# Seven half-size products in place of eight in two of the six gate/up blocks of each FFN

## The chip, the core and the metric

One core of a Trainium2 chip runs the whole program in one launch. The metric is the device time in microseconds (us). The engines are TensorE (PE in the profile: matmuls, with weight loads on a row of their own, PEld), VectorE (DVE), ScalarE (ACT), GpSimd (POOL) and SyncE (SP), whose queue issues the DMA transfers.

## The reference

Two layers, each of an FFN, a mixer and a second FFN, on 256 tokens of width 1024. The inner width of an FFN is 2816.

```python
def swiglu(h, w_gate, w_up, w_down):
    return (jax.nn.silu(h @ w_gate) * (h @ w_up)) @ w_down

for l in range(DEPTH):
    f1 = swiglu(rmsnorm(x, g[0]), ffn_w_gate[l, 0], ffn_w_up[l, 0], ffn_w_down[l, 0])
    x = x + 0.5 * rmsnorm(f1, g[1])
    m = hybrid_mixer(rmsnorm(x, g[2]), ...)   # S5 scan, chunk attention, gates
    x = x + rmsnorm(m, g[3])
    f2 = swiglu(rmsnorm(x, g[4]), ffn_w_gate[l, 1], ffn_w_up[l, 1], ffn_w_down[l, 1])
    x = x + 0.5 * rmsnorm(f2, g[5])
```

## The kernel before

The 256 tokens are two tiles of 128. All weights stream from DRAM once, in 368 chunks of 128 x 1024 fp32 (512 KB each). `weight` brings a chunk in: a DMA into a `raw` buffer, an ACT copy to `wh` in a format with fewer bits that PE reads (L358), and a DVE subtraction `wl` = `raw` - `wh` (L365), whose two inputs both lie in SBUF. A product of fp32 quality is then three matmuls: high by high, high by low and low by high. `mm_two_k` does this for a chunk that holds two 128-row pieces of a 512-wide block: six matmuls 128x512 (L400). Both token tiles use each chunk, tile 1 some three chunks after tile 0 (`LAG`).

An FFN goes through its inner width in blocks, `N_BLK`: five of 512 and one of 256. For a block of 512 a tile takes four gate chunks and four up chunks, 24 matmuls each; DVE multiplies the up result with the SiLU of the gate result, `t_split` transposes it on PE (L414) and splits it into high and low, and `gemm_wide` takes it through the four down chunks of the block before, into two PSUM banks per tile that hold the FFN's output until the end.

The order is no hand-written one: `Kern` records operations with an estimated cost, and `Graph.schedule` places them by due times (a clock of `TAU` per half chunk, less `MARGIN` for work of another stream) and by free buffers. `SLOTS` is the number of buffers of each kind. On each engine instructions then run strictly in that order. GpSimd does little: some memsets, and the power -1/2 of the norms (`pow`, L376, 128x1). Small work for the mixer (`prep`) is strewn over the first FFN of a layer, or over the FFN in front of it.

Of the kernel before, what the change touches and what calls it, by code (L numbers as in the profile page):

```python
# [12 lines left out]
F32 = mybir.dt.float32  # L13
# [7 lines left out]
P = 128  # L21
# [8 lines left out]
N_BLK = (512, 512, 512, 512, 512, 256)  # L30
FFN_CHUNKS = 66
# [4 lines left out]
SLOTS = {"blk": 28, "ps": 8, "wh": 8, "wl": 8, "raw": 4, "gain": 2,  # L36
# [4 lines left out]
MARGIN = {"conv": 7.558, "conv0": 3.423, "task": 7.748, "att0": 37.576, "s50": 37.749, "att1": 28.585, "s51": 29.753, "prep": 111.598}  # L41
# [20 lines left out]
class View:  # L62
# [249 lines left out]
class Kern:  # L312
    def __init__(self, g, x, g0, gains, wall, sp, bias, out):
# [4 lines left out]
        self.chunk = [0, 0]  # L318
        self.last_raw = None
# [46 lines left out]

    def copy(self, out, a):
# [24 lines left out]
    def mm(self, out, lhsT, rhs, start, stop):  # L392
        n, m = rhs.free_size(), lhsT.free_size()
        if rhs.dt == F32R:
            cost = n / 2370
        elif m == 32:
            cost = 0.05
        else:
            cost = max(0.2, n / 592)
        return self.g.op("pe", cost, [out], [lhsT, rhs], lambda: self.nc.tensor.matmul(  # L400
            out.ap(), lhsT=lhsT.ap(), rhs=rhs.ap(), start=start, stop=stop))
# [40 lines left out]

    def weight(self, i):
        if i not in self.ws:
# [3 lines left out]
            raw = g.buf("raw", [P, 1024])  # L448
            wh, wl = g.buf("wh", [P, 1024], F32R), g.buf("wl", [P, 1024], F32R)
            parts = [slice(0, 512), slice(512, 1024)] if i < 2 else [slice(0, 1024)]  # L450
            for s in parts:
                self.last_raw = self.dma(raw[:, s], self.w_d[i][:, s], after=[self.last_raw] if self.last_raw else [])
            for s in parts:
                self.act(wh[:, s], raw[:, s], AF.Copy)
                self.tt(wl[:, s], raw[:, s], wh[:, s].bitcast(F32), ALU.subtract)
            self.ws[i] = (wh, wl)
# [3 lines left out]
    def take(self, t):  # L460
# [16 lines left out]
    def gemm(self, t, xs):
# [6 lines left out]
        return bank  # L484

# [658 lines left out]
```

## Time and profile before

| | |
|---|---|
| time, median of 3 runs | 1153.3 us (1153.28 to 1153.45) |
| span of the profiled execution, first to last instruction | 1151.6 us |
| granted TensorE clock | 0.999 of full speed |
| PE busy | 1140.8 us, 99% |
| DVE busy | 788.6 us, 68% |
| ACT busy | 606.3 us, 53% |
| POOL busy | 19.8 us, 2% |

The page gives no time of the profiled execution beside its span; the span is 1.7 us below the median of the runs, and that much lies around it. Busy shares are means over stages that differ: FFN blocks, boundaries and mixers alternate.

### The profile page before, as it was taken

What the parts mean: (1) busy time and instruction counts of PE and PEld (TensorE: products, weight loads), DVE (VectorE), ACT (ScalarE), POOL (GpSimd) and SP (SyncE); (2) the same over time, 40 slices, a digit from 0 to 9 for tenths busy, and PEclk for the clock granted to TensorE, in tenths of its full rate; (3) what the DMA queues carried; (4) which work ended last, traced back from release to release, by engine and by line L of the source; (5) the groups of instructions that cost most, each with busy time, mean ns of one, the idle gap of its engine ahead of it and who ended that gap; (6) DMA issues with size and microseconds to landing.
All of it is one profiled execution on the core that took longest, in us unless ns stands there. A gap on an engine that the chain in (4) does not pass through costs nothing.

```text
span 1151.6 us, 15538 instructions
## 1 busy us (share of the span) xinstructions
PE 1140.8 (99%) x5872; PEld 914.0 (79%) x5872; DVE 788.6 (68%) x1190; ACT 606.3 (53%) x894; POOL 19.8 (2%) x53
## 2 busy tenths in 40 slices
PE   8999999999999999999999999999999999999997
PEld 7887888877788888888888878887777888888886
DVE  6995557896958854655799734578779678544553
ACT  6565445648555554444555643455685446444442
POOL 1000000000000000000000000000000000000000
PEclk9999999999999999999999999999999999999999
DMA  8754565553255665555565546654534565555551
GB/s 291 252 195 159 183 219 166 181 164 130 86 189 178 207 200 184 186 182 184 187 220 193 184 150 200 204 177 147 166 110 145 184 198 163 192 192 181 190 165 37
DMA packets 60267, 205.02 MB, mean 178 GB/s; under 512 B 7072, under 2 KB 7840, under 8 KB 60192
## 3 DMA queue, kind: packets, MB, share of 16 engines
q1 hardware_dynamic: 60192, 204.03, 53.7%
q8 instruction: 46, 0.75, 0.3%
q14 instruction: 29, 0.24, 0.1%
HBM read 202.96 MB, written 1.05 MB: 177 GB/s over the span
## 4 chain that ended last, share of the span: by engine, by line
PE 94%; ACT 4%; issue 1%; DMA 0%; SPq 0%; DVE 0%; POOLq 0%; POOL 0%; DVEq 0%
PE ps L400 89%; PE ps L414 4%; ACT utz L358 2%; PE ps L406 1%; ACT blk L358 1%; ACT wh L358 1%; DMA x<-in_x_dram 0%; SPq L341 0%; DVE x L380 0%; POOLq L1139 0%; POOL s L376 0%; DVEq L1139 0%; DVE s L388 0%; POOLq L376 0%
## 5 line engine op out<-in xcount | busy, mean ns | idle before, releaser
L400 PE MATMUL ps<-wh,blk 128*128 128x512 f32 x2944 | 916.4, 400 | 0.0
L400 PEld LDWEIGHTS ps<-wh,blk 128*128 128x128 f32 x2944 | 548.0, 188 | 122.6 <-issue 0.3
L365 DVE TENSOR_TENSOR wl<-raw,wh 128x1024 fp32r<-128x1024 f32 (+1 forms) x370 | 448.7, 1217 | 281.9 <-ACT wh L358 280.6
L358 ACT ACTIVATE wh<-raw 128x1024 fp32r<-128x1024 f32 (+1 forms) x370 | 389.7, 1055 | 374.5 <-PE ps L400 334.1
L400 PE MATMUL ps<-wl,blk 128*128 128x512 f32 x1472 | 551.7, 399 | 0.0
L400 PEld LDWEIGHTS ps<-wl,blk 128*128 128x128 f32 x1472 | 274.8, 188 | 61.1 <-issue 0.3
L358 ACT ACTIVATE blk<-ps 128x512 fp32r<-128x512 f32 (+3 forms) x136 | 78.1, 583 | 121.5 <-PE ps L414 103.3
L365 DVE TENSOR_TENSOR blk<-ps,blk 128x512 fp32r<-128x512 f32 (+2 forms) x104 | 69.0, 666 | 36.1 <-ACT blk L358 34.9
L414 PE MATMUL ps<-ident,blk 128*128 128x128 f32 x432 | 76.8, 273 | 0.2
L414 PEld LDWEIGHTS ps<-ident,blk 128*128 128x128 f32 x432 | 57.0, 140 | 20.1 <-ACT blk L358 1.0
L358 ACT ACTIVATE blk<-ps,s 128x512 f32<-128x512 f32 (+1 forms) x80 | 52.5, 658 | 27.6 <-PE ps L400 25.6
L380 DVE SCALAR_TENSOR_TENSOR blk<-ps,s,blk 128x512 f32<-128x512 f32 (+1 forms) x48 | 33.8, 703 | 15.3 <-PE ps L400 11.5
L376 POOL TENSOR_TENSOR s<-s,mhalf 128x1 f32<-128x1 f32 x24 | 13.8, 574 | 804.0 <-DVE s L388 799.1
L358 ACT ACTIVATE blk<-blk,s 128x128 f32<-128x128 f32 (+1 forms) x64 | 25.8, 444 | 0.0
L400 PEld LDWEIGHTS ps<-utz,bt 128*128 128x128 f32 x128 | 18.1, 191 | 4.0 <-ACT utz L358 2.8
L365 DVE TENSOR_TENSOR blk<-blk,blk 128x512 f32<-128x512 f32 (+3 forms) x38 | 21.1, 577 | 0.1
L358 ACT ACTIVATE utz<-blk 32x128 f32<-32x128 f32 x64 | 20.1, 314 | 1.0
L358 ACT ACTIVATE blk<-blk 64x128 f32<-64x128 f32 (+2 forms) x44 | 17.1, 393 | 6.5 <-DVE blk L380 6.0
L365 DVE TENSOR_TENSOR blk<-blk,e 128x512 f32<-128x512 f32 x32 | 20.3, 677 | 0.0
L400 PE MATMUL ps<-utz,bt 128*128 128x128 f32 x128 | 19.2, 278 | 1.0 <-ACT utz L358 0.8
L365 DVE TENSOR_TENSOR blk<-ps,e 128x512 f32<-128x512 f32 x32 | 19.9, 677 | 0.0
L856 DVE TENSOR_TENSOR_SCAN blk<-mt,blk 128x512 f32<-128x512 f32 x16 | 18.6, 1203 | 0.0
(106 smaller groups left out, 349.2 us busy)
## 6 DMA issues: line engine op xcount, KB each, us to landing
raw<-in_wall_dram SPq DMA_DIRECT2D x366, 512.0 KB, 3.5
gain<-in_gains_dram SPq DMA_DIRECT2D x22, 256.0 KB, 4.6
blk<-in_bias_dram SPq DMA_DIRECT2D x8, 256.0 KB, 5.0
raw<-in_wall_dram SPq DMA_DIRECT2D x4, 256.0 KB, 3.5
blk<-in_sp_dram SPq DMA_DIRECT2D x4, 256.0 KB, 4.0
x<-in_x_dram SPq DMA_DIRECT2D x3, 256.0 KB, 5.5
out_dram<-x SPq DMA_DIRECT2D x2, 256.0 KB, 2.0
out_dram<-x SPq DMA_DIRECT2D x2, 192.0 KB, 2.1
```

What stands on the lines that cost most here:

```text
L358: self.nc.scalar.activation(out=out.ap(), in_=in_.ap(), func=func, **k)
L365: lambda: self.nc.vector.tensor_tensor(out=out.ap(), in0=a.ap(), in1=b.ap(), op=op))
L376: lambda: self.nc.gpsimd.tensor_tensor(out=out.ap(), in0=a.ap(), in1=b.ap(), op=ALU.pow))
L380: return self.g.op("dve", cost, [out], [a, s, b], lambda: self.nc.vector.scalar_tensor_tensor(out=out.ap(), in0=a.ap(), scalar=ap(s), in1= ...
L400: return self.g.op("pe", cost, [out], [lhsT, rhs], lambda: self.nc.tensor.matmul(out.ap(), lhsT=lhsT.ap(), rhs=rhs.ap(), start=start, stop ...
L406: self.nc.tensor.matmul(out.ap(), lhsT=lhsT.ap(), rhs=rhs.ap(), start=start, stop=stop)
L414: lambda o=o, s=s: self.nc.tensor.transpose(o.ap(), s.ap(), self.ident.ap()))
L856: self.g.op("dve", 0.6, [o], [mt, z], lambda o=o, z=z: self.nc.vector.tensor_tensor_scan(out=o.ap(), data0=mt.ap(), data1=z.ap(), initial= ...
```

## The change

In blocks 1 and 3 of each FFN (`SEVEN`) the two token tiles are computed together. With A11, A12 the two halves of tile 0's normed input along its 1024 columns, A21, A22 those of tile 1, and B11, B21 the gate weights and B12, B22 the up weights of the same halves, the gate and up results of both tiles are eight products of half size. `seven` forms them from seven: `p1` = A11 B11, then A12 B21, and five products of sums of A with differences of B; DVE adds the parts up out of PSUM (`u2`, `u4`, `h`). Each product is two chunks, 12 matmuls, so a block takes 84 in place of 96 for gate and up, and 48 as before for the down part. The sums of A (`sums`) are built once per FFN by GpSimd from the high and low parts, eight operations of 128x512, and split again by ACT and DVE. The differences of B are built per block by GpSimd in place in the raw buffers, eight operations of 128x1024 (`ptt`), and each difference needs its own ACT copy and DVE subtraction: 14 converted chunks for gate and up where there were 8.

Around it: 9 raw buffers for 4, and 7 each of `wh` and `wl` for 8; the chunks of these blocks lie in DRAM in the order of use; due times after a block move up by `saved`; `ffn` records both tiles; the zeroed buffers `utz` of the S5 part become blocks that GpSimd clears in each mixer.

```diff
+SEVEN = (1, 3)
...
-SLOTS = {"blk": 28, "ps": 8, "wh": 8, "wl": 8, "raw": 4, "gain": 2,
+SLOTS = {"blk": 28, "ps": 8, "wh": 7, "wl": 7, "raw": 9, "gain": 2,
...
+    def ptt(self, out, a, b, op):
+        return self.g.op("pool", 0.1 + a.free_size() * 0.0022, [out], [a, b],
+                         lambda: self.nc.gpsimd.tensor_tensor(out=out.ap(), in0=a.ap(), in1=b.ap(), op=op))
...
+    def halves(self, raw, parts=(slice(0, 1024),)):
+        wh, wl = self.g.buf("wh", [P, 1024], F32R), self.g.buf("wl", [P, 1024], F32R)
+        for s in parts:
+            self.act(wh[:, s], raw[:, s], AF.Copy)
+            self.tt(wl[:, s], raw[:, s], wh[:, s].bitcast(F32), ALU.subtract)
+        return wh, wl
...
-        self.mode("main", "main", (i + t * min(LAG, 1 + i // 2)) * 2 * TAU + t * TAU)
+        self.mode("main", "main", (i + t * min(LAG, 1 + i // 2)) * 2 * TAU + t * TAU - self.saved)
...
+    def wide_step(self, banks, x, w, first):
+        for n in range(2):
+            s = slice(n * 512, (n + 1) * 512)
+            self.mm(banks[n], x[0], w[0][:, s], first, False)
+            self.mm(banks[n], x[0], w[1][:, s], False, False)
+            self.mm(banks[n], x[1], w[0][:, s], False, False)
...
-    def ffn(self, t, l, f, normed):
+    def sums(self, xs):
+        self.mode("sums", "bulk")
+        a = []
+        for t in range(2):
+            for hi, lo in xs[t].full:
+                r = self.blk()
+                self.ptt(r, hi.bitcast(F32), lo.bitcast(F32), ALU.add)
+                a.append(r)
+        a11, a12, a21, a22 = a
+        self.ptt(a22, a21, a22, ALU.add)
+        self.ptt(a21, a11, a21, ALU.subtract)
+        self.ptt(a11, a22, a11, ALU.subtract)
+        self.ptt(a12, a12, a11, ALU.subtract)
+        out = []
+        for r in (a22, a11, a21, a12):
+            hi, lo = self.blk(F32R), self.blk(F32R)
+            self.split((r, hi, lo))
+            out.append((hi, lo))
+        self.mode()
+        return out
+
+    def seven(self, b, xs, rs, s, acc, pend, first):
...
+        self.saved += 2 * TAU
...
+        b11 = [self.load(i), self.load(i + 1)]
+        w1 = conv(b11)
+        self.weight(i + 2)
+        b21 = [self.load(i + 3), self.load(i + 4)]
+        w2 = conv(b21)
+        b12 = [self.load(i + 5), self.load(i + 6)]
+        for u in range(2):
+            self.ptt(b11[u], b12[u], b11[u], ALU.subtract)
+        w5 = conv(b11)
+        b22 = [self.load(i + 7), self.load(i + 8)]
+        for u in range(2):
+            self.ptt(b11[u], b22[u], b11[u], ALU.subtract)
+        w6 = conv(b11)
+        self.weight(i + 9)
+        for u in range(2):
+            self.ptt(b12[u], b22[u], b12[u], ALU.subtract)
+        w7 = conv(b12)
+        w3 = conv(b22)
+        self.weight(i + 10)
+        for u in range(2):
+            self.ptt(b21[u], b21[u], b11[u], ALU.subtract)
+        w4 = conv(b21)
+        self.weight(i + 11)
...
+        p1 = self.ps()
+        prod(0, p1, a11, w1, True)
+        k1 = self.blk()
+        self.act(k1, p1, AF.Copy)
+        down(2, 0)
+        prod(4, p1, a12, w2, False)
+        sil = [self.blk(), self.blk()]
+        self.act(sil[0], p1, AF.Silu, scale=rs[0])
+        p5, p6 = self.ps(), self.ps()
+        prod(6, p5, s1, w5, True)
+        prod(8, p6, s2, w6, True)
+        u2, u4 = self.blk(), self.blk()
+        self.tt(u2, p6, k1, ALU.add)
+        self.tt(u4, p5, u2, ALU.add)
+        down(10, 1)
+        p7 = self.ps()
+        prod(12, p7, s3, w7, True)
+        self.tt(u4, p7, u4, ALU.add)
+        prod(14, p5, s4, w3, False)
+        h = [self.blk(), u4]
+        self.tt(h[0], p5, u2, ALU.add)
+        self.stt(h[0], h[0], rs[0], sil[0], ALU.mult, ALU.mult)
+        down(16, 2)
+        prod(18, p7, a22, w4, False)
+        self.tt(u2, p7, u2, ALU.add)
+        self.act(sil[1], u2, AF.Silu, scale=rs[1])
+        self.stt(h[1], h[1], rs[1], sil[1], ALU.mult, ALU.mult)
+        down(20, 3)
+        return [self.t_split(h[t], 4) for t in range(2)]
...
-        for t in self.CT + [self.D0] + self.uTz:
+        for t in self.CT + [self.D0]:
...
+        uz = [self.blk() for _ in range(2)]
+        for z in uz:
+            self.memset("pool", z, 0.0)
...
-            normed = [self.ffn(t, l, 0, normed[t]) for t in range(2)]
+            normed = self.ffn(l, 0, normed)
```

On GpSimd, before, there were eight `pow` and nothing else from the end of layer 0's mixer through both FFNs that follow it; the first five of them:

```order
L376 TENSOR_TENSOR s1_667_3634<-s1_666_3627,mhalf_2_74 128x1
L376 TENSOR_TENSOR s1_781_3740<-s1_780_3732,mhalf_2_74 128x1
L376 TENSOR_TENSOR s1_677_3786<-s1_676_3781,mhalf_2_74 128x1
L376 TENSOR_TENSOR s1_791_3859<-s1_790_3856,mhalf_2_74 128x1
L376 TENSOR_TENSOR s1_1047_5163<-s1_1046_5156,mhalf_2_74 128x1
```

With the change, in block 1 of layer 0's second FFN alone (raw_888 and raw_889 are the two chunks of B11, raw_897 and raw_898 of B21, raw_903 and raw_904 of B12, raw_909 and raw_910 of B22; the 128x512 rows belong to `sums`):

```order
L377 TENSOR_TENSOR blk_879_3919<-blk_878_3897,blk_879_3919 128x512
L377 TENSOR_TENSOR raw_888_3663<-raw_903_3781,raw_888_3663 128x1024
L377 TENSOR_TENSOR raw_889_3690<-raw_904_3802,raw_889_3690 128x1024
L377 TENSOR_TENSOR blk_878_3897<-blk_876_3833,blk_878_3897 128x512
L377 TENSOR_TENSOR raw_903_3781<-raw_909_3842,raw_903_3781 128x1024
L377 TENSOR_TENSOR raw_888_3663<-raw_909_3842,raw_888_3663 128x1024
L377 TENSOR_TENSOR raw_889_3690<-raw_910_3931,raw_889_3690 128x1024
L377 TENSOR_TENSOR blk_876_3833<-blk_879_3919,blk_876_3833 128x512
L377 TENSOR_TENSOR raw_904_3802<-raw_910_3931,raw_904_3802 128x1024
L377 TENSOR_TENSOR blk_877_3882<-blk_877_3882,blk_876_3833 128x512
L377 TENSOR_TENSOR raw_897_3746<-raw_897_3746,raw_888_3663 128x1024
L377 TENSOR_TENSOR raw_898_3767<-raw_898_3767,raw_889_3690 128x1024
```

The queue has gone from `pow` alone to all sums and differences of the block in one row, and the last two, which make B21 - (B22 - B12 + B11) for the last product, stand behind all others.

On DVE before, in block 1 of the same FFN, the low parts alternate with the SwiGLU products and the splits:

```order
L365 TENSOR_TENSOR wl_852_3945<-raw_850_3891,wh_851_3936 128x1024
L365 TENSOR_TENSOR wl_858_3967<-raw_856_3902,wh_857_3960 128x1024
L365 TENSOR_TENSOR blk_824_3989<-ps_822_3973,blk_823_3982 128x512
L365 TENSOR_TENSOR wl_861_3996<-raw_859_3916,wh_860_3987 128x1024
L365 TENSOR_TENSOR wl_864_4012<-raw_862_3934,wh_863_4003 128x1024
L365 TENSOR_TENSOR wl_867_4032<-raw_865_3958,wh_866_4023 128x1024
L380 SCALAR_TENSOR_TENSOR blk_826_4041<-ps_840_3956,s1_677_3786,blk_825_3949 128x512
L365 TENSOR_TENSOR wl_873_4058<-raw_871_3978,wh_872_4047 128x1024
L365 TENSOR_TENSOR blk_1066_4068<-ps_1064_4051,blk_1065_4061 128x512
L365 TENSOR_TENSOR wl_876_4082<-raw_874_4006,wh_875_4075 128x1024
L365 TENSOR_TENSOR wl_879_4100<-raw_877_4021,wh_878_4093 128x1024
L380 SCALAR_TENSOR_TENSOR blk_1068_4113<-ps_1070_4034,s1_791_3859,blk_1067_4030 128x512
```

With the change, in the same block (wl_919, wl_912, wl_914 and wl_921 are low parts of differences that GpSimd has made):

```order
L373 TENSOR_TENSOR wl_919_4078<-raw_903_3781,wh_918_4056 128x1024
L373 TENSOR_TENSOR blk_875_4092<-ps_873_4068,blk_874_4074 128x512
L373 TENSOR_TENSOR wl_912_4099<-raw_888_3663,wh_911_4083 128x1024
L373 TENSOR_TENSOR blk_883_4113<-blk_876_3833,blk_882_4105 128x512
L373 TENSOR_TENSOR wl_914_4121<-raw_889_3690,wh_913_4110 128x1024
L373 TENSOR_TENSOR wl_923_4131<-raw_909_3842,wh_922_4118 128x1024
L373 TENSOR_TENSOR wl_921_4143<-raw_904_3802,wh_920_4128 128x1024
L373 TENSOR_TENSOR blk_887_4156<-blk_877_3882,blk_886_4149 128x512
L373 TENSOR_TENSOR wl_925_4163<-raw_910_3931,wh_924_4137 128x1024
L373 TENSOR_TENSOR wl_928_4175<-raw_926_4081,wh_927_4153 128x1024
L373 TENSOR_TENSOR blk_942_4185<-ps_941_4134,blk_937_4041 128x512
L373 TENSOR_TENSOR wl_935_4190<-raw_933_4096,wh_934_4166 128x1024
```

Subtractions whose `raw` input GpSimd has just written now stand among those that only wait for a DMA and ACT, and additions out of PSUM (blk_942) stand behind them.

## Rows read from the trace of the kernel before

**Rows 1.** The page's busy time, share of the span and instructions of each engine.

```profile
PE 1140.8 (99%) x5872; PEld 914.0 (79%) x5872; DVE 788.6 (68%) x1190; ACT 606.3 (53%) x894; POOL 19.8 (2%) x53
```

**Rows 2.** Who waited for whom, TensorE alone: total us, times, longest.

```profile
PE ps L414 <- DMA x<-in_x_dram: 2.0, 2, 1.8
PE ps L1015 <- POOL mhalf L346: 1.4, 1, 1.4
PE ps L400 <- ACT utz L358: 0.8, 2, 0.4
```

**Rows 3.** Chain that ended last, 425 to 540 us: start, us, what.

```profile
429.88 23.69 PE ps L400 x102
453.57 0.22 PE ps L414 x2
...
522.94 9.03 PE ps L400 x39
```

**Rows 4.** Stretches: length, busy us (count) by engine, clock, DMA share, GB/s.

```profile
0.00:60.00 60.00, 56.65 (x254) 45.63 (x255) 47.79 (x138) 36.13 (x54) 5.33 (x21) 1.00 0.78 269
60.00:120.00 60.00, 60.00 (x327) 47.31 (x326) 42.26 (x79) 36.12 (x59) 0.00 (x0) 1.00 0.53 172
...
425.00:458.50 33.50, 33.50 (x151) 27.06 (x150) 16.58 (x17) 15.07 (x16) 0.00 (x0) 1.00 0.56 181
```

**Rows 5.** Waits of all engines: total us, times, longest.

```profile
ACT wh L358 <- PE ps L400: 334.1, 237, 3.0
```

**Rows 6.** DVE groups by form: busy us, mean ns | idle before.

```profile
L365 DVE TENSOR_TENSOR wl<-raw,wh 128x1024 fp32r<-128x1024 f32 x366 | 446.0, 1223 | 278.9 <-ACT wh L358 277.7 <-issue 0.3
L365 DVE TENSOR_TENSOR blk<-ps,blk 128x512 fp32r<-128x512 f32 x76 | 52.3, 688 | 28.5 <-ACT blk L358 27.6
L380 DVE SCALAR_TENSOR_TENSOR blk<-ps,s,blk 128x512 f32<-128x512 f32 x40 | 29.9, 748 | 11.7 <-PE ps L400 11.5
...
L365 DVE TENSOR_TENSOR blk<-blk,pt_ar 128x256 f32<-128x256 f32 x8 | 3.3, 418 | 0.0
```

**Rows 7.** ACT groups by form, the same columns.

```profile
L358 ACT ACTIVATE wh<-raw 128x1024 fp32r<-128x1024 f32 x366 | 387.2, 1059 | 371.6 <-PE ps L400 334.1 <-issue 15.8 <-DMA raw<-in_wall_dram 14.6
...
L358 ACT ACTIVATE blk<-ps 128x512 fp32r<-128x512 f32 x76 | 45.4, 597 | 87.6 <-PE ps L414 83.6 <-PE ps L406 4.0
```

**Rows 8.** POOL groups by form, the same columns.

```profile
L376 POOL TENSOR_TENSOR s<-s,mhalf 128x1 f32<-128x1 f32 x24 | 13.8, 574 | 804.0 <-DVE s L388 799.1 <-DVE blk L365 4.9
L346 POOL MEMSET ct<- 128x512 f32 x4 | 2.0, 528 | 0.0
...
L346 POOL MEMSET st<- 128x16 f32 x4 | 0.4, 131 | 61.9 <-PE ps L406 61.9
```

**Rows 9.** Timeline of POOL, 765 to 779 us: start, us, instruction.

```profile
766.10 0.55 POOL L376 TENSOR_TENSOR s<-s,mhalf 128x1 f32<-128x1 f32 x1 [43.98 <-DVE s L388]
777.35 1.11 POOL L376 TENSOR_TENSOR s<-s,mhalf 128x1 f32<-128x1 f32 x1 [10.70 <-DVE s L388]
```

**Rows 10.** Timeline of DVE around the first of these.

```profile
765.87 0.68 DVE L365 TENSOR_TENSOR blk<-ps,blk 128x512 f32<-128x512 f32 x1
766.47 0.68 DVE L365 TENSOR_TENSOR blk<-ps,gain 128x512 f32<-128x512 f32 x1
```

**Rows 11.** Timeline of DVE around the second.

```profile
775.49 1.23 DVE L365 TENSOR_TENSOR wl<-raw,wh 128x1024 fp32r<-128x1024 f32 x1 [0.26 <-ACT wh L358]
776.64 0.21 DVE L388 TENSOR_SCALAR s<-s 128x1 f32<-128x1 f32 x1
776.77 0.68 DVE L365 TENSOR_TENSOR blk<-ps,blk 128x512 f32<-128x512 f32 x1
777.37 0.68 DVE L365 TENSOR_TENSOR blk<-x,gain 128x512 f32<-128x512 f32 x1
778.49 0.75 DVE L380 SCALAR_TENSOR_TENSOR blk<-blk,s,blk 128x512 f32<-128x512 f32 x1 [0.44 <-POOL s L376]
```

More of the change, by code (lines that the diff above doesn't have):

```diff
@@ L390, in ts, with mm @@
         return self.g.op("dve", cost, [out], [a, s1], fn)
-    def mm(self, out, lhsT, rhs, start, stop):
+    def mm(self, out, lhsT, rhs, start, stop, again=False):
         n, m = rhs.free_size(), lhsT.free_size()
@@ L399, in mm @@
             cost = max(0.2, n / 592)
+        kw = {"skip_group_check": True} if again else {}
         return self.g.op("pe", cost, [out], [lhsT, rhs], lambda: self.nc.tensor.matmul(
-            out.ap(), lhsT=lhsT.ap(), rhs=rhs.ap(), start=start, stop=stop))
+            out.ap(), lhsT=lhsT.ap(), rhs=rhs.ap(), start=start, stop=stop, **kw))
     def mm_group(self, cost, mms):
@@ L447, in weight @@
             self.mode("conv" if i >= 6 else "conv0", "main")
[L448 to L456, printed above, removed]
+            parts = (slice(0, 512), slice(512, 1024)) if i < 2 else (slice(0, 1024),)
+            self.ws[i] = self.halves(self.load(i, parts), parts)
             g.stream, g.rank, g.due = keep
@@ L522, in to_lhs @@
         self.split(*trios)
-        return [p for h in range(2) for p in zip(self.cols(nh[h]), self.cols(nl[h]))]
+        return Lhs(nh, nl, [p for h in range(2) for p in zip(self.cols(nh[h]), self.cols(nl[h]))])
     def row_scale(self, t, after=()):
@@ new lines, in seven, with conv, prod, down @@
+    def seven(self, b, xs, rs, s, acc, pend, first):
+        i = self.chunk[0]
+        assert self.chunk == [i, i]
+        self.chunk = [i + 12, i + 12]
+        t0 = i * 2 * TAU - self.saved
+        self.saved += 2 * TAU
+        for t in range(2):
+            for n in range(12):
+                self.mark[(t, i + n)] = len(self.g.ops)
+        def conv(raws):
+            return [self.halves(r) for r in raws]
+        self.mode("conv", "main")
+        b11 = [self.load(i), self.load(i + 1)]
[21 more added lines that the diff above has]
+        self.weight(i + 11)
+        def prod(at, bank, a, w, start):
+            self.mode("main", "main", t0 + at * TAU)
+            pairs = list(zip(self.cols(a[0]), self.cols(a[1])))
+            for u in range(2):
+                self.mm_two_k(bank, pairs[2 * u:2 * u + 2], w[u], start and u == 0, u == 1, not start)
+            self.mode()
+        def down(at, c):
+            for t in range(2):
+                self.mode("main", "main", t0 + (at + t) * TAU)
+                self.wide_step(acc[t], pend[t][c], self.weight(i + (2, 9, 10, 11)[c]), first and c == 0)
+            self.mode()
+        (a11, a12), (_, a22) = xs[0].full, xs[1].full
+        s1, s2, s3, s4 = s
+        p1 = self.ps()
[27 more added lines that the diff above has]
+        return [self.t_split(h[t], 4) for t in range(2)]
@@ L599, in ffn @@
                     self.gain(*nxt)
-            if b == len(N_BLK) - 1:
-                pre = self.pre_gain(t, *nxt)
-            if pend is not None:
-                self.gemm_wide(t, acc, pend, first, False)
-                first = False
-            pend = res
-        self.gemm_wide(t, acc, pend, False, True)
-        return self.boundary(t, l, ipost, acc, 1.0 / 16, 4.0 * EPS, *nxt, pre)
+        out = []
+        for t in range(2):
+            self.gemm_wide(t, acc[t], pend[t], False, True)
+            out.append(self.boundary(t, l, ipost, acc[t], 1.0 / 16, 4.0 * EPS, *nxt, pre[t]))
+        return out
     def persistent(self):
@@ L1080, in _ffn_chunks @@
     for i in range(1, len(N_BLK)):
-        out += [gu[i], dn[i - 1]]
+        if i in SEVEN:
+            out += [gu[i][:2], dn[i - 1][:1], gu[i][2:], dn[i - 1][1:]]
+        else:
+            out += [gu[i], dn[i - 1]]
     out.append(dn[-1])
```

68 lines of the change are left out of this document (47 added, 21 removed).

## The prediction

> **What bounds the kernel now.** I read the busy shares first: TensorE is busy for 1140.8 of 1151.6 us, DVE for 68%, ACT for 53%, GpSimd for 2% [rows 1]. Next come TensorE's own waits: three lines, 4.2 us together, two of them at the start [rows 2]. The chain of waits shows what a filled TensorE costs: 102 matmuls in 23.69 us and 39 in 9.03 us, 0.2323 and 0.2315 us each, with two transposes in 0.22 us [rows 3]. I take 0.2324 for a matmul and 0.11 for a transpose. So TensorE sets the end, and whatever takes matmuls away shortens the program as long as the weights come in time. Weights are made ahead: ACT's longest wait is for buffers that TensorE still reads, 334.1 us in 237 waits [rows 5]. How much room the makers have is read from stretches: over one FFN block without other work (33.5 us) DVE is busy 16.6 us and ACT 15.1, but in the first 60 us, where the small work of `prep` is done, DVE is busy 47.8 [rows 4].
>
> **What is removed.** Eight blocks lose 12 matmuls each, 96 in all: 96 x 0.2324 = 22.3 us. TensorE has no gap that could swallow that; if nothing else waits, the time is 1153.3 - 22.3 = 1131.0 us. (The profiled execution spans 1151.6 us; the 1.7 us to the median lie around it and stay.) The number of transposes and of bytes is unchanged, and the DMA engines are 56% busy in a clean block [rows 4], so I cost the shorter block at nothing there; the nine raw buffers let transfers start sooner, and behind a late subtraction they would start later.
>
> **What is added.** Per block, ACT makes six more copies of 1.059 us [rows 7], so 18 of them plus five evictions of 0.6 [rows 7]: 22 us in a block that now has 132 matmuls and 8 transposes, 31.6 us. That fits. DVE makes six more subtractions of 1.223 us, and five more operations on PSUM of 0.69 to 0.75 [rows 6]: 18 x 1.223 + 9 x 0.7 = 28.3 of 31.6 us. That fits too, barely, and only if nothing slows DVE. GpSimd gets eight subtractions of 128x1024 per block and eight of 128x512 per FFN; no row has one of that size. Bounds for one: a memset of 128x512 takes 0.528 us and one of 128x16 0.131 [rows 8], so one pass costs 0.8 ns per column, and 1024 columns 0.94 us. That is the least. An operation that reads two inputs one after the other makes two passes, 1.75 us; with the write as a third, 2.55. I take the middle of these two, 2.15 us (1.13 for 512 columns). By themselves eight of them are 17 us of 31.6 and fit.
>
> **Where they meet.** The dearest point is whether GpSimd and DVE can do this at the same time. Two rows answer in part. The `pow` at 766.10 us, started while DVE worked on an operation with one input in PSUM [rows 10], took 0.55 us; the one at 777.35 took 1.11 [rows 9]. In the second case DVE had at 777.37 begun a product of `x` and `gain`, both in SBUF, which ran to 778.05 [rows 11]. The mean over all 24 is 574 ns [rows 8], so this one stands alone, and it is the one that met a DVE operation with two SBUF inputs. I read it as GpSimd being shut out until DVE had done. The subtractions that make `wl` are of that kind, all of them. No row shows the reverse, DVE behind a long GpSimd operation; I take it to hold, since one shared way in would serve one of them at a time.
>
> The Trainium skill says the same and more (SBUF — State Buffer, section on who interferes with whom): a DVE instruction with two SBUF inputs contends with a GpSimd instruction that reads SBUF, and whoever starts first holds the shared ports for its whole instruction. The 1.11 us against 0.55 agrees for GpSimd as the loser; the other direction no run here shows yet.
>
> **The sum.** If they exclude each other, their times add. I count, in the written order of the changed kernel, from a block's first difference on GpSimd to the low part of its last product (the two rows that stand last in GpSimd's queue feed it), and beside it what TensorE does from that first difference to the last product's first matmul. In block 1 of layer 0's second FFN these are: DVE 16 subtractions of 1.223 and 4 of 0.684 on split sums, 22.3 us, less about 1 us because an operation right behind another starts 0.08 us before the other's row ends (775.49 to 776.64 for a row of 1.23) [rows 11]; GpSimd 8 x 2.15 + 3 x 1.13 = 20.6; together 41.9. TensorE: 145 matmuls and 8 transposes, 34.6. The last product is 7.3 us late. Operations of DVE that read PSUM are left out, since GpSimd may run beside them. For all eight blocks in order, TensorE has 32.9, 40.3, 34.6, 37.4, 34.6, 38.9, 34.6 and 37.4 us (138 to 162 matmuls each); DVE's two-input work, less 1 us each, is 25.8, 34.2, 21.3, 22.5, 20.3, 28.9, 21.3 and 18.6 (dearer where `prep` is strewn in, for instance 24 operations of 128x256 at 0.418 in the second [rows 6]); GpSimd has 17.2 plus 1.1, 0, 3.4, 0, 3.4, 0, 3.4 and 0. The shortfalls are 11.2, 11.2, 7.3, 2.3, 6.3, 7.3, 7.3 and none: 52.9 us. What waits is TensorE, in order, for a `wh` or `wl` of the products 5, 6, 7 and 4; behind it stand the down chunks of the same block. Between the blocks the makers catch up, since a normal block uses half of DVE. So 1153.3 - 22.3 + 52.9 = 1183.9, say **1184 us**.
>
> With two passes (1.75 us) the shortfalls sum to 29.4 and the time is 1160; with three (2.55) 78.9 and 1210; with the memset's pace (0.94) 2.4 and 1133. The Trainium skill (GPSIMD Engine Reference, section on performance versus the Vector engine) has a two-input add of 2048 fp32 columns at 4497 ns, from which I estimate 2.25 us for 1024; by that figure the shortfalls would be 58.4 and the time 1189. No row here has such an operation.
>
> The rest I cost at nothing, with its cover: seven `wh`/`wl` for eight, covered by the 334.1 us that ACT waits for buffers [rows 5], worth one chunk (2.3 us of making) less of lead; eight memsets of 0.53 us [rows 8] in the mixers on an idle GpSimd; keeping the tiles in step, which changes no matmul.
>
> **Rivals.** *GpSimd gives way alone.* DVE goes on while GpSimd waits; each difference costs 2.15 and at most one DVE row, 1.22, so 8 x 3.4 = 27 us in 33 to 40: no product is late, and the time is 1131, at most 1133 (the second block has 35.2 us of two-input work and 6.5 of other DVE work against 40.3). For it: the one row that shows the clash shows GpSimd as the loser. Against it: that `pow` was the one that came second, or nearly so, and so tells nothing of a GpSimd operation that came first. It lies on the other side, and would show as `wl` rows of an unchanged 1.22 us. I give it 0.28.
>
> *They exclude each other, but a difference is short.* Between 0.94 us (2.4 us lost) and 1.75 (29.4), the gain of 22.3 is used up at about 1.54 us. Below that the kernel is faster or the same, 1133 to 1153. Speaking against it: `pow` needs 0.55 us for a single column, so GpSimd isn't quick at two-input work. I give it 0.12: 0.07 faster, 0.05 the same.
>
> *ACT is the one held up.* Copies of differences wait for GpSimd in ACT's queue, in front of the evictions of `p1` and of transposes that TensorE needs soon. Without any clash of ports, a pair of differences that lands one pair late (2 x 2.15 us) in each of the eight blocks, and isn't covered, costs 34 us and gives 1165. Against it: 16 to 21 us of TensorE's work lie between a block's last difference and its use. I give it 0.05.
>
> That the change doesn't remove what it says is no rival: the built program has 96 matmuls 128x512 fewer.
>
> **The numbers.** The forecast has 0.55 and its own range is 1160 to 1210. The three rivals have 0.28, 0.12 and 0.05. Faster by over 0.2% (2.3 us, about what a measurement of this kernel can tell) are the first rival and part of the second, 0.35; the same 0.05; slower 0.60. Cases of both signs hold much of the chance, so the range goes from 1130 to 1210: the first rival's time at one end, three passes at the other.
>
> **What the profile will show.** If I am right: rows of GpSimd's differences or of `wl` beside them longer than alone (2.15 and 1.22), by up to the other's length; TensorE waits of some microseconds for `wh` or `wl` in blocks 1 and 3 and hardly elsewhere, most where `prep` falls; the chain of waits going through GpSimd's line and `wl` there. A TensorE busy share still at 99% would refute the sum. I would be wrong if DVE keeps its 1.22 us beside a running difference, or if a difference takes well under 1.5 us.

## The result and the profile after

The changed kernel takes 1258.5 us (median of 4 runs, 1257.6 to 1260.0) against 1153.4 for the kernel before, run beside it: a ratio of 1.091 (95% interval 1.090 to 1.093). The side was right, and so was the clash of GpSimd and DVE; the size was not, and 1258 lies well above the range, which ended at 1210. Of the predicted sum, 1153.3 - 22.3 + 52.9, the last term should have been 127.5.

The page's busy row of the changed kernel, beside [rows 1]: TensorE has its 96 matmuls less, and is busy for 16 us longer. DVE has gained 226 us for 104 instructions more.

```profile
PE 1156.7 (92%) x5776; PEld 916.3 (73%) x5776; DVE 1014.3 (81%) x1294; ACT 663.2 (53%) x966; POOL 276.7 (22%) x155
```

TensorE's waits, beside [rows 2] (total us, times, longest). They were 4.2 us; now DVE is the releaser of 82, with operations of three kinds: the SwiGLU products in front of transposes (L392), low parts (wl) and operations that read PSUM (blk L373; additions are 6.9 us of these 9.4, the splits of transposes nearly all the rest).

```profile
PE ps L427 <- DVE blk L392: 42.4, 12, 7.5
PE ps L413 <- DVE wl L373: 30.4, 10, 7.0
PE ps L413 <- DVE blk L373: 9.4, 8, 2.9
```

Groups of GpSimd and DVE by form, beside [rows 6] and [rows 8] (busy us, mean ns | idle before). Low parts took 1223 ns and take 1450, `pow` 574 and now 907. A DVE operation with an input in PSUM has kept its time, 685 for 688.

```profile
L377 POOL TENSOR_TENSOR raw<-raw,raw 128x1024 f32<-128x1024 f32 x64 | 183.0, 2872 | 232.8 <-DMA raw<-in_wall_dram 86.6 <-DVE wl L373 81.8 <-DVE pt_fr L373 43.1
L377 POOL TENSOR_TENSOR blk<-blk,blk 128x512 f32<-128x512 f32 x32 | 64.3, 2012 | 41.7 <-DVE blk L373 25.6 <-DVE blk L392 12.2 <-DVE s L400 3.7
L388 POOL TENSOR_TENSOR s<-s,mhalf 128x1 f32<-128x1 f32 x24 | 21.7, 907 | 563.1 <-DVE s L400 469.9 <-PE ps L413 93.3
...
L373 DVE TENSOR_TENSOR wl<-raw,wh 128x1024 fp32r<-128x1024 f32 x414 | 591.2, 1450 | 179.4 <-ACT wh L366 175.1 <-DMA raw<-in_wall_dram 1.7 <-DMA gain<-in_gains_dram 1.5
L373 DVE TENSOR_TENSOR blk<-ps,blk 128x512 fp32r<-128x512 f32 x76 | 51.9, 685 | 17.8 <-ACT blk L366 15.4 <-PE ps L413 1.1
```

Where it is lost is read from the eight stretches of the prediction's sum, each from a block's first difference on GpSimd to the first matmul of the last product's second chunk, which is where the prediction's counts end too (length, busy us and count by engine, clock, DMA share, GB/s).

```profile
32.40:78.40 46.00, 32.67 (x123) 25.12 (x122) 44.53 (x36) 20.10 (x25) 27.26 (x10) 0.81 0.47 159
107.00:167.10 60.10, 47.91 (x252) 36.14 (x251) 58.91 (x73) 36.13 (x59) 23.04 (x8) 0.91 0.32 119
439.10:487.00 47.90, 35.73 (x137) 27.12 (x135) 47.12 (x31) 23.96 (x29) 29.75 (x12) 0.86 0.37 129
515.70:564.30 48.60, 40.35 (x165) 32.00 (x164) 47.23 (x64) 22.60 (x25) 20.85 (x8) 0.89 0.38 139
...
sum 403.10, PE 313.79 PEld 242.46 DVE 389.87 ACT 205.71 POOL 204.99; mean PE 39.22 PEld 30.31 DVE 48.73 ACT 25.71 POOL 25.62
```

TensorE stands still for 403.1 - 313.8 = 89.3 us. The trace has 1146 matmuls and 80 transposes there, 275.1 us at 0.2324 and 0.109; the other 38.7 us of its busy time is nearly all the lower granted clock (0.81 to 0.93; 128 tiny matmuls of `prep` are in it too). Together 128.0 us, of 129 that the profiled execution (1260.0 us) lost: nearly the whole loss lies in these stretches, as the prediction had it. And DVE is busy for 389.9 of the 403.1 us, where a row that stands behind GpSimd counts as busy.

Three timelines of the third stretch, GpSimd, DVE and TensorE (start, us, instruction), show how it goes.

```profile
437.86 1.29 POOL L377 TENSOR_TENSOR blk<-blk,blk 128x512 f32<-128x512 f32 x1
439.12 5.24 POOL L377 TENSOR_TENSOR raw<-raw,raw 128x1024 f32<-128x1024 f32 x2
...
446.55 3.34 POOL L377 TENSOR_TENSOR raw<-raw,raw 128x1024 f32<-128x1024 f32 x1
...
456.12 2.35 POOL L377 TENSOR_TENSOR raw<-raw,raw 128x1024 f32<-128x1024 f32 x1 [2.35 <-issue]
```

```profile
442.01 3.43 DVE L373 TENSOR_TENSOR wl<-raw,wh 128x1024 fp32r<-128x1024 f32 x1
445.36 0.68 DVE L373 TENSOR_TENSOR blk<-ps,blk 128x512 fp32r<-128x512 f32 x1
445.96 5.01 DVE L373 TENSOR_TENSOR wl<-raw,wh 128x1024 fp32r<-128x1024 f32 x2
450.89 0.68 DVE L373 TENSOR_TENSOR blk<-blk,blk 128x512 fp32r<-128x512 f32 x1
451.49 4.49 DVE L373 TENSOR_TENSOR wl<-raw,wh 128x1024 fp32r<-128x1024 f32 x2
455.91 0.74 DVE L392 SCALAR_TENSOR_TENSOR blk<-ps,s,blk 128x512 f32<-128x512 f32 x1
```

```profile
449.69 0.50 PE L413 MATMUL ps<-wh,blk 128*128 128x512 f32 x1 [2.30 <-ACT blk L366]
...
456.70 1.11 PE L427 MATMUL ps<-ident,blk 128*128 128x128 f32 x4 [5.67 <-DVE blk L392]
...
458.04 1.48 PE L413 MATMUL ps<-wh,blk 128*128 128x512 f32 x3
```

The low part at 442.01 takes 3.43 us: GpSimd's two differences run until 444.36, and the 1.08 us from there to its end is nearly the 1.22 that it takes alone. This is the direction that no row of before had: DVE behind a GpSimd operation that had started first. The other direction stands in the difference at 446.55: it takes 3.34 us, behind a low part that had begun before it, where the one at 456.12, beside a SwiGLU product that reads PSUM, takes 2.35. The Trainium skill's rule (SBUF — State Buffer, section on who interferes with whom: the loser is blocked until the winner's instruction ends) holds here in both directions. Then four more low parts take 9.50 us among GpSimd's next operations, where four alone take 4.9, and behind them, in DVE's order, the SwiGLU product at 455.91, for which TensorE waits 5.67 us with four transposes (it belongs to the block before). After that wait the three matmuls from 458.04 stand 0.43 us apart in place of 0.23, the lower of the clock's two levels.

The chain of waits over the same stretch (start, us, what) is DVE's for 38 us, with little between its pieces but "issue" (time in which the profile shows no wait), until an addition out of PSUM at 479.19 lets TensorE go: the next product adds to the bank that this addition reads.

```profile
442.01 3.43 DVE wl L373
445.44 0.60 DVE blk L373
...
479.19 0.61 DVE blk L373
479.80 0.14 issue
479.94 10.25 PE ps L413 x43
```

Not every stretch ends like this one. The rows show TensorE's last wait in the third stretch, and in the fourth:

```profile
479.94 0.47 PE L413 MATMUL ps<-wh,blk 128*128 128x512 f32 x1 [1.21 <-DVE blk L373]
...
546.33 0.80 PE L413 MATMUL ps<-wl,blk 128*128 128x512 f32 x1 [7.03 <-DVE wl L373]
```

In the third, fifth, seventh and eighth stretch the last wait over 0.3 us is for such an addition, with 7 to 10 us of TensorE's own work behind it. In the first, second, fourth and sixth it is earlier, for a low part of product 6, with 13 to 18 us of TensorE's own work behind it.

### The profile page after: what moved, and what is told of

It is laid out like the page before. It is cut to its first block, busy times and chain, and to the rows that moved or that the text cites. A ratio compares the mean times of both kernels' runs of the same rounds, so it can differ in the third digit from the quotient of the medians.

```text
span 1258.2 us, 15762 instructions
## 1 busy us (share of the span) xinstructions
PE 1156.7 (92%) x5776; PEld 916.3 (73%) x5776; DVE 1014.3 (81%) x1294; ACT 663.2 (53%) x966; POOL 276.7 (22%) x155
## 4 chain that ended last, share of the span: by engine, by line
PE 59%; DVE 27%; issue 6%; ACT 5%; POOL 2%; DMA 1%; SPq 0%; POOLq 0%; DVEq 0%; ACTq 0%
PE ps L413 56%; DVE wl L373 14%; DVE blk L373 7%; ACT blk L366 3%; PE ps L427 2%; ACT wh L366 2%; DVE blk L392 1%; PE ps L419 1%; DMA raw<-in_wall_dram 1%; DVE blk L1001 1%; DVE x L392 1%; POOL blk L377 1%; DVE e L373 1%; POOL raw L377 1%; DMA gain<-in_gains_dram 0%
## 5 line engine op out<-in xcount | busy, mean ns | idle before, releaser
L413 PE MATMUL ps<-wh,blk 128*128 128x512 f32 x2880 | 905.9, 407 | 16.5 <-DVE blk L373 9.4
L373 DVE TENSOR_TENSOR wl<-raw,wh 128x1024 fp32r<-128x1024 f32 (+1 forms) x418 | 594.0, 1443 | 182.5 <-ACT wh L366 178.2
L366 ACT ACTIVATE wh<-raw 128x1024 fp32r<-128x1024 f32 (+1 forms) x418 | 432.3, 1053 | 375.3 <-PE ps L413 298.5
L413 PE MATMUL ps<-wl,blk 128*128 128x512 f32 x1440 | 543.9, 407 | 30.5 <-DVE wl L373 30.4
L377 POOL TENSOR_TENSOR raw<-raw,raw 128x1024 f32<-128x1024 f32 x64 | 183.0, 2872 | 232.8 <-DMA raw<-in_wall_dram 86.6
L427 PE MATMUL ps<-ident,blk 128*128 128x128 f32 x432 | 80.3, 290 | 45.1 <-DVE blk L392 42.4
L373 DVE TENSOR_TENSOR blk<-ps,blk 128x512 fp32r<-128x512 f32 (+2 forms) x144 | 96.3, 670 | 25.6 <-ACT blk L366 22.7
L377 POOL TENSOR_TENSOR blk<-blk,blk 128x512 f32<-128x512 f32 x32 | 64.3, 2012 | 41.7 <-DVE blk L373 25.6
L366 ACT ACTIVATE blk<-blk 32x128 f32<-32x128 f32 (+3 forms) x124 | 47.4, 383 | 30.0 <-POOL blk L377 15.3
L373 DVE TENSOR_TENSOR blk<-blk,blk 128x512 fp32r<-128x512 f32 (+3 forms) x54 | 43.8, 835 | 4.8 <-ACT blk L366 4.7
L366 ACT ACTIVATE blk<-blk,s 128x128 f32<-128x128 f32 (+2 forms) x72 | 31.7, 473 | 5.3 <-DVE blk L373 4.1
L392 DVE SCALAR_TENSOR_TENSOR blk<-blk,s,blk 128x512 f32<-128x512 f32 x36 | 29.8, 834 | 1.0 <-ACT blk L366 0.8
L392 DVE SCALAR_TENSOR_TENSOR blk<-ps,s,blk 128x512 f32<-128x512 f32 (+1 forms) x32 | 21.7, 678 | 3.0 <-PE ps L413 1.8
L392 DVE SCALAR_TENSOR_TENSOR x<-blk,s,x 128x512 f32<-128x512 f32 (+2 forms) x26 | 20.7, 822 | 0.1
```

The lines of the kernel that those rows point to most:

```text
L366: self.nc.scalar.activation(out=out.ap(), in_=in_.ap(), func=func, **k)
L373: lambda: self.nc.vector.tensor_tensor(out=out.ap(), in0=a.ap(), in1=b.ap(), op=op))
L377: lambda: self.nc.gpsimd.tensor_tensor(out=out.ap(), in0=a.ap(), in1=b.ap(), op=op))
L392: return self.g.op("dve", cost, [out], [a, s, b], lambda: self.nc.vector.scalar_tensor_tensor(out=out.ap(), in0=a.ap(), scalar=ap(s), in1= ...
L427: lambda o=o, s=s: self.nc.tensor.transpose(o.ap(), s.ap(), self.ident.ap()))
```

## The experiments

Diffs are against the changed kernel unless another is named; ratios are to the kernel before, timed beside each.

### 1. The rest of the change, without the blocks

```diff
-SEVEN = (1, 3)
+SEVEN = ()
```

> The changed kernel with no block made from seven products: 9 raw and 7 wh/wl buffers, both tiles recorded together and the cleared blocks of the mixer stay. Theory (GpSimd's two-input operations and DVE's shut each other out): nothing of that is left, 1151 to 1157 us. Rival A (late results of a slow GpSimd, no clash): the same. Rival B (the seven-product block itself is too much for ACT, DVE and the PSUM banks): the same. Rival C (the buffers, or tiles in step): well above 1160, towards 1258.

1157.0 us, 1.003 (1.001 to 1.005). Buffers, DRAM order, `utz` and tiles in step cost 3.4 us, where the prediction had nothing; the rest belongs to the blocks.

### 2. No work on GpSimd

```diff
 def ptt(self, out, a, b, op):
-    return self.g.op("pool", ...)
+    pass
```

> The changed kernel without any sum or difference on GpSimd: the products use the plain weights and high parts of the inputs, so the output is another; all 14 conversions a block, the splits and the additions out of PSUM stay. Theory: TensorE is full, 1131 to 1140 us, wl rows back at 1.22 us. Rival A: the same. Rival B: TensorE still waits in blocks 1 and 3, 1200 to 1258 us.

1136.5 us, 0.985 (0.982 to 0.988). So ACT's copies, DVE's low parts and additions fit, and the 122 us between this and the changed kernel are GpSimd's sums and differences and what they do to others. The first rival (1131) would have had them cost next to nothing. DVE's low parts by form:

```profile
L373 DVE TENSOR_TENSOR wl<-raw,wh 128x1024 fp32r<-128x1024 f32 x414 | 495.9, 1223 | 202.7 <-ACT wh L366 201.1
```

### 3. Two memsets for each sum and difference

```diff
-    lambda: self.nc.gpsimd.tensor_tensor(out=out.ap(), in0=a.ap(), in1=b.ap(), op=op))
+    lambda: [self.nc.gpsimd.memset(out.ap(), 0.01) for _ in range(2)])
```

> The changed kernel with two memsets of the same place (about 0.95 us each for 1024 columns) in place of each sum and difference: GpSimd is busy nearly as long and ACT and DVE wait for it as before, but it reads nothing; the output is another. Theory: 1131 to 1145 us, wl rows at 1.22 us. Rival A (lateness of the results): still 1200 to 1258. Rival B: 1200 to 1258.

1140.8 us, 0.989 (0.986 to 0.992). GpSimd by form, and DVE beside it:

```profile
L377 POOL MEMSET raw<- 128x1024 f32 x128 | 120.6, 956 | 213.5 <-DVE wl L373 113.7 <-DMA raw<-in_wall_dram 84.1 <-DVE pt_mag L373 12.0
L377 POOL MEMSET blk<- 128x512 f32 x64 | 33.1, 527 | 1.9
...
L373 DVE TENSOR_TENSOR wl<-raw,wh 128x1024 fp32r<-128x1024 f32 x414 | 497.0, 1223 | 203.3 <-ACT wh L366 200.4 <-DMA gain<-in_gains_dram 1.5
```

GpSimd works 154 us here, in the same places, and everybody who waited for its results still waits for these; only the reading is gone. The time is 4 us above run 2 and low parts take 1223 ns. That a late GpSimd holds up ACT (the third rival) is not what costs.

### 4. GpSimd work that nobody waits for, in the kernel before

```diff
+    if 8 <= j < 16 or 32 <= j < 40:
+        self.g.op("pool", 2.35, [self.scr], [wl, wh], lambda: self.nc.gpsimd.tensor_tensor(
+            out=self.scr.ap(), in0=wl.bitcast(F32).ap(), in1=wh.bitcast(F32).ap(), op=ALU.add))
```

> The kernel before, with one GpSimd addition wl + wh (128x1024) into a spare buffer that nobody reads, behind each of the eight gate and up chunks of blocks 1 and 3: 64 in all. Theory: wl rows beside them last up to 3.4 us, TensorE waits, 1165 to 1230 us. Rival A: nothing waits for these results, so 1152 to 1156 us and wl rows of 1.22. Rival B: 1152 to 1156.

1175.9 us, 1.019 (1.016 to 1.022). Sixty-four additions 128x1024 whose result is never read cost 22 us in a kernel whose DVE is half idle in a clean block [rows 4]. Low parts rise to 1408 ns, nearly as in the changed kernel. One of the additions that met nobody:

```profile
481.14 2.40 POOL L460 TENSOR_TENSOR scr<-wl,wh 128x1024 f32<-128x1024 f32 x1 [37.53 <-DVE wl L366]
```

So an operation alone takes 2.35 to 2.40 us; the prediction's 2.15 was 9% short, and the second rival (under 1.54 us) is out.

### 5. Sums and differences on DVE

```diff
-    return self.g.op("pool", 0.1 + a.free_size() * 0.0022, [out], [a, b], ...)
+    return self.tt(out, a, b, op)
```

> The changed kernel with all sums and differences on DVE in place of GpSimd (0.68 us for 512 columns, 1.22 for 1024), planned so. Theory (GpSimd's reads and DVE's two-input reads shut each other out, and the GpSimd operation is the longer one, 2.36 us): although DVE gets all of GpSimd's work, 1145 to 1175 us; DVE's load by the rows leaves some 29 us of lateness in the three blocks beside prep, so 1160. Rival (a difference costs the same wherever it is made, since late weights are what counts): 1220 to 1258.

1190.5 us, 1.032 (1.030 to 1.034): between the two expectations and neither. With nobody to clash with, every DVE operation keeps its time (1222 ns for a difference), and 90 us of added DVE work (961.2 us busy for 871.7 in run 2) still cost 54 us more than run 2. This was the first sign that the clash is half the story: what is full is DVE's queue (in this run's third stretch DVE is busy for 41.7 of 43.7 us, with no clash).

### 6. Sums and differences in quarters

```diff
+    n = a.free_size() // 4
+    for i in range(4):
+        s = slice(i * n, (i + 1) * n)
+        self.nc.gpsimd.tensor_tensor(out=out[:, s].ap(), in0=a[:, s].ap(), in1=b[:, s].ap(), op=op)
```

> The changed kernel with each sum and difference cut into four GpSimd instructions of a quarter of the columns, in the same place of the order. Theory in its long form (besides the sum of the times, DVE stands behind a whole GpSimd instruction, and the operations that TensorE needs next stand behind that in DVE's order): no wl row over 2.2 us and less time lost than with whole ones, 1190 to 1235 us. Rival (only the sum of port times counts): the same sum and some more fixed cost, 1255 to 1270 us.

1266.0 us, 1.098 (1.095 to 1.100): the time that the rival gave, but the run doesn't decide between the two. The first half of the theory came true: no wl row is over 1.82 us (up to 3.45 with whole differences), and in the third stretch DVE stands idle for 14 of 51.4 us, where it had 0.8 of 47.9. But GpSimd's work grew. A quarter takes 0.72 us or a little more where it meets nobody and 1149 ns on average, where one of four parts of 2.36 us would be 590; the four together take 4.6 us, where a whole difference in the changed kernel takes 2.87. GpSimd is now the busiest, 43.9 of the 51.4 us, and ACT waits 69.8 us for its differences where it waited 15.1.

```profile
L380 POOL TENSOR_TENSOR raw<-raw,raw 128x256 f32<-128x256 f32 x256 | 285.0, 1149 | 165.5 <-DMA raw<-in_wall_dram 71.6 <-DVE wl L373 46.1 <-DVE pt_fr L373 34.8
439.85:491.25 51.40, 37.55 (x137) 28.36 (x136) 37.22 (x31) 24.08 (x29) 43.92 (x45) 0.87 0.37 130
```

So cutting the operations up doesn't pay here, and what one long hold costs by itself stays open.

### 7. An order planned with the clash

```diff
+    if e == "pool" and o.cost > 1.2:
+        free["dve"] = max(free["dve"], o.end)
```

> The changed kernel with the same operations, but the planner counts DVE as taken while a GpSimd sum or difference runs, so that the order on all engines allows for it. Theory in its long form (the part of the loss above the sum of the times, some 60 of 118 us, comes from an order made without the clash): 1180 to 1215 us. Rival (only the sum of port times counts, whatever the order): 1240 to 1265 us.

1262.6 us, 1.095 (1.092 to 1.097). The scheduler now counts the two as one, and this other order of the same work gains nothing. It is one order; that no order would gain is not shown.

### 8. One block in place of two, its sums on DVE

```diff
-SEVEN = (1, 3)
+SEVEN = (4,)
-    return self.g.op("pool", ...)
+    return self.tt(out, a, b, op)
-    cost = n / 2370
+    cost = n / 2203
```

> Seven products in block 4 alone of each FFN, where no prep stands, with sums and differences on DVE and the planner's cost of a matmul set to the 0.232 us of the rows (n/2203 in place of n/2370). 48 matmuls fewer are worth 11.2 us, the other parts of the change cost 3.4 (run e1). Theory: DVE has 36 of some 35 us of work in that block and half a block's room before it, so TensorE hardly waits: 1143 to 1150 us. Rival (late weights): 1155 or more.

1148.9 us (5 runs, 1148.7 to 1149.6), 0.996 (0.995 to 0.998): 0.4% faster than the kernel before, and even the end of the interval lies beyond the 0.2% that the prediction took as what can be told.

Its 48 matmuls fewer are worth 11.2 us; 6.6 are given back, 3.4 of them by what run 1 measured.

### 9. A third of the seven products' matmuls left out

```diff
-    self.mm(bank, xl, wh[:, i * 512:(i + 1) * 512], False, last and i == len(xs) - 1, again)
+    self.mm(bank, xl, wh[:, i * 512:(i + 1) * 512], False, last and i == len(xs) - 1, again, live)
...
-    self.mm_two_k(bank, pairs[2 * u:2 * u + 2], w[u], start and u == 0, u == 1, not start)
+    self.mm_two_k(bank, pairs[2 * u:2 * u + 2], w[u], start and u == 0, u == 1, not start, False)
```

> Every seventh of TensorE's work less: of the seven products the third matmul of each set of three (low part of the input by high part of the weights) is left out, 28 of 84 in each of the eight blocks, 224 in all, some 52 us at 0.232 us each; the output is another one. All other engines do what they did, in the same order. If TensorE's end is set by the shared port over the whole stretch (the theory of the prediction, only with a larger sum), the matmuls left out only turn into waiting and the time stays at 1240 us or more. If TensorE waits early in a stretch and then does the rest as its own work (theory of the early wait), each matmul left out behind that wait counts: 1195 to 1230 us, as 28 matmuls are 6.5 us a block and some of them stand before the wait.

1246.3 us, 1.080 (1.077 to 1.084). 52 us less of TensorE's work shorten the program by 12. TensorE's waits grew in their place, those for low parts from 30.4 to 43.0, those for operations that read PSUM from 9.4 to 19.2:

```profile
PE ps L413 <- DVE wl L373: 43.0, 12, 8.9
PE ps L427 <- DVE blk L392: 42.6, 12, 7.5
PE ps L413 <- DVE blk L373: 19.2, 11, 4.3
```

The theory of one early wait in every stretch, with TensorE the bound behind it, falls. The third, fifth and seventh stretch keep their 48 us to 0.1: there DVE's queue sets the pace to the end. The other five are shorter by 1.5 to 2.7 us each, 10.9 of the 12: there some of the matmuls left out did stand behind the last wait.

### 10 to 12. Parts of GpSimd's work

Run 10 leaves out the differences of the products 7 and 4, run 11 turns the sums of A into memsets, run 12 leaves out all differences and keeps the sums.

```diff
+    def ptt(self, out, a, b, op, live=True):
...
-    self.ptt(b12[u], b22[u], b12[u], ALU.subtract)
+    self.ptt(b12[u], b22[u], b12[u], ALU.subtract, False)
```

> The differences for the products 7 and 4 (B12 - B22 and the last one, four of the eight per block) are left out, so these two products use unmade weights and the output is another one; order, copies and low parts stay. This is half of GpSimd's work, and the half that the last product waits for. By the sum as the prediction took it, at the last product, four differences of 2.36 us less remove the shortfall of nearly every stretch: 1140 to 1165 us. By the theory of the early wait the first four differences and the sums of A are what TensorE waits for, and much of the loss stays: 1190 to 1230 us.

> The eight sums of A per FFN (128x512, on GpSimd) become memsets of the same tiles, so the output is another one; all differences of B stay. Sums fall only into the first of the two blocks of an FFN, four stretches in all. By the sum at the last product this takes 3 x 1.27 us off each of three stretches and little off the first: about 12 us, 1245 to 1250. By the theory of the early wait all eight stand in front of TensorE's first wait (1.27 us each and what they hold up on DVE): 20 to 36 us, 1222 to 1238.

> The other half of the last one: all eight differences of B per block are left out (the output is another one), the sums of A stay on GpSimd, order and all copies and low parts stay. Both theories: with 32 operations of 128x512 left, 41 us of GpSimd, most of the loss goes: 1140 to 1165. What it tells is the price of the sums by themselves: 1136 would be nothing, over 1165 that they alone make a third of the loss.

In that order they took 1192.3 us (1.034, 1.031 to 1.037), 1234.0 (1.070, 1.067 to 1.073) and 1153.2 (1.000, 0.999 to 1.001). All three lie where the theory of the early wait put them, though run 9 had spoken against it; a queue that is full throughout would give such numbers too, since it counts work wherever it stands in a stretch. Work here is 2.36 us for an operation of 1024 columns and 1.27 for one of 512, what each takes where it meets nobody:

| run | GpSimd operations | us of work | over run 2 (1136.5) | per us of work |
|---|---|---|---|---|
| 12 | 32 of 512 | 41 | 16.7 | 0.41 |
| 10 | 32 of 1024, 32 of 512 | 116 | 55.9 | 0.48 |
| 11 | 64 of 1024 | 151 | 97.6 | 0.65 |
| changed kernel | 64 of 1024, 32 of 512 | 192 | 122.0 | 0.64 |
| 5 (on DVE) | none; 96 operations on DVE | 90 of DVE | 54.0 | 0.60 |

The first of the work fits into DVE's gaps, the rest costs nearly its length: from run 10 to the changed kernel 76 us of work cost 66.

### 13. Transposes that wait for nothing

```diff
-    self.transpose_into(bank, self.cols(src, nkt))
+    self.transpose_into(bank, self.cols(src, nkt), self.cols(self.x[t]))
```

> The transposes at the end of each FFN block read the residual in place of the SwiGLU product, so they wait for no DVE product (42 us of TensorE's waits in the changed kernel); the output is another one, and all instructions and their order stay. If TensorE's waits count one by one, most of the 42 us go and some of the time at the lower clock with them: 1195 to 1220 us. If DVE's in-order queue is what is full through the whole stretch, TensorE runs on to the next low part or addition and waits there: 1240 us or more, with the waits for DVE's low parts and additions grown by most of the 42.

1262.3 us, 1.094 (1.091 to 1.097). TensorE's largest wait is gone (L392 from 42.4 us to 0.6) and the program is no shorter. The waiting has moved to the next operations that read PSUM in DVE's queue (30.7 us for 9.4; low parts stay at 30.3), and to ACT's copies ahead of the transposes (16.7 on L428):

```profile
PE ps L413 <- DVE blk L373: 30.7, 9, 7.0
PE ps L413 <- DVE wl L373: 30.3, 13, 8.1
PE ps L428 <- ACT blk L366: 16.7, 4, 8.0
...
PE ps L428 <- DVE blk L392: 0.6, 3, 0.2
```

### 14. Three additions out of PSUM done three times

```diff
-    self.tt(u2, p6, k1, ALU.add)
+    self.tt(u2, p6, k1, ALU.add, 3)
```

> Three of the five additions out of PSUM of each of the eight blocks are done three times over (same operands, same result): 48 more DVE operations of 0.6 us from one start to the next, 29 us, of the kind that the prediction left out of its sum because GpSimd may run beside them. If that holds: no more than 5 us longer, up to 1264. If DVE's queue is full through the stretch and these additions come behind GpSimd's last difference, they count in full: 1275 to 1290 us.

1287.9 us, 1.117 (1.113 to 1.120): 29.4 us for 48 operations, 0.61 each. They count in full, over the program as a whole; by stretch the six cost 1.9 to 5.5 us. TensorE's wait for operations that read PSUM is 28.6 us where it was 9.4:

```profile
PE ps L414 <- DVE blk L373: 28.6, 10, 5.8
```

## Why the prediction was right in kind and wrong in size

**Removed work.** Right: run 2, with the matmuls gone and no GpSimd work, comes to 1136.5, which is 1131.0 plus the 3.4 of run 1 and 2 more.

**The clash.** Right, and in both directions (3.43 us for a low part, 3.34 for a difference). Run 3 shows that it hangs on GpSimd reading, run 4 that it needs nobody to wait for the result. On GpSimd that only writes the Trainium skill says the same (SBUF — State Buffer, section on who interferes with whom), and run 3 agrees with 1223 ns.

**The length of a difference.** 2.15 us was taken and 2.36 measured, 1.13 and 1.27 for 512 columns. The estimate of 2.25 us from the Trainium skill (GPSIMD Engine Reference, section on performance versus the Vector engine) was 5% short of the same rows. With this and a little more, the port's time from the first difference to the low part of the last product, which the prediction had at 342 us over the eight stretches (TensorE's times and shortfalls added, the last one 35.8), is 358 in the trace. This term was mis-sized by 16 us, and the third stretch's 41.9 is 42.9.

**The sum.** This is the step that failed: "The last product is 7.3 us late", a shortfall formed once, at the low part of the last product, between the port's time and TensorE's. Measured are 17.0 us of loss in that stretch (47.9 long, 30.9 of work), and 128 in all for 51 (52.9 with the last one set to none). In order the eight lose 18.1, 19.8, 17.0, 11.5, 16.5, 18.8, 16.8 and 9.5. Besides the 16 us above two things were wrong with it:

- It gave TensorE 290.7 us of work beside the port, from the written order. It had 275.1 left: 15.6 us. A recount in the order in which the kernel emits its operations, up to the same matmul, gives 281.6 (27.9 for 32.9 in the first stretch), so 9.1 of the 15.6 were miscounted; by the other 6.5 TensorE was further on at a first difference than the order says.
- It ended the stretch at the wrong operation. The matmuls of the last product's second chunk start 45 us later, over eight stretches, than their low part is ready. They start 42 us later in the runs 10 and 12 too, where less or little is lost: low parts are simply made that far ahead. What TensorE waits for last comes out of DVE's queue earlier: in four stretches an addition out of PSUM that stands behind low parts (479.19 in the third stretch), in the other four a low part of product 6. Then 7 to 18 us of TensorE's own work follow. DVE's queue and this work follow one another, where the sum laid them side by side.

16.4 + 15.6 + 44.6 = 76.6, and 51.3 + 76.6 = 127.9, against 128.0. The three add up to the loss by the way they are formed: they say where the sum departs from the trace, not what each costs by itself.

**"Operations of DVE that read PSUM are left out."** Wrong for the ones that matter. Some do run beside GpSimd: the splits at 445.36 and the SwiGLU product at 455.91 do. But the additions come behind the last difference, in the same full queue, and 48 more of them cost 0.61 us each on average (run 14). Whether GpSimd could work beside them mattered little: DVE has one queue, and it was that queue that was full, as run 5 shows without any clash.

**The clock.** The sum had no term for it. Behind its longer waits (5.67 us before 456.70) TensorE's matmuls stand 0.43 us apart for a while; in the eight stretches that makes nearly all of 38.7 us of the 128, against none in the forecast. It is contained in the three terms above, since they were counted in time that passed, and no run separates it. Run 9 points the same way: with 52 us of matmuls fewer, standing still grew, and the granted clock fell from 0.961 to 0.950.

**What would show.** Waits only in blocks 1 and 3, right (89.3 of 101.5 us of idle time). Most where `prep` falls, right by a little: 18.1, 19.8 and 18.8 us in the three stretches where most of it falls, against 16.5 to 17.0 in the other three of block 1 and 11.5 and 9.5 in the other two of block 3. A chain through `wl`, right; through GpSimd's own line, hardly (2%), since a low part that stands behind GpSimd is booked as DVE's.

**Rest at nothing.** 3.4 us (run 1); in the changed kernel itself only 1 us of the loss lies outside the eight stretches.

Open is how much of the loss a plan with more `wh` and `wl` buffers would save, since ACT's copies wait for those that TensorE still reads (298.5 us in all); it was not tried, and the one other order that was (run 7) gave nothing. Open too is the cost of one long hold (run 6).

## What to carry to other kernels

Before work is put on an idle GpSimd, ask whether it reads SBUF while DVE runs operations with two SBUF inputs: if so, add both to one queue, and compare its whole length, operations on PSUM included, with the time of the engine that sets the end. Where that queue is the longer one, don't form the shortfall at the last operand; find, stretch by stretch, the last result in the queue for which the engine waits, and add the work that this engine still has behind it. And where TensorE begins to wait, its lower clock comes on top: here nearly all of 38.7 us beside 89.3 of standing still.

## What was not expected of the hardware

- Standing still cost TensorE again in clock: in the eight stretches 89.3 us in waits of up to 7.5 us came with 38.7 us, nearly all lost to the lower level. Over the whole program run 9 stood still for 129 us, the changed kernel for 101.5, and run 9's granted clock was 0.950 for 0.961.
- Cutting GpSimd's operations to a quarter relieved DVE (956.5 us busy for 1014.3) and gained nothing: GpSimd was busy for 399 us in place of 277, and the end came 7 us later.
- GpSimd can stand behind more than one DVE operation. One difference, at 115.77 us in the second stretch, took 5.14 us, while DVE ran nine operations of 128x256 with two SBUF inputs one right behind another (from 115.61 to 118.71); it is the only difference that took over 3.5 us.
- GpSimd's memsets beside low parts held up neither side's operations (956 ns for 128x1024, low parts 1223), and the time was 4 us above run 2.
